# Down products of a feed-forward accumulated in shared PSUM banks, two token tiles at a time

## The chip, the cores and the metric

One Trainium2 chip, one core of it. The metric is the device time of one execution in microseconds (us), as the median of several runs. In rows and text PE is the matrix engine, DVE the vector engine, ACT the scalar engine, POOL GpSimd, and SP the queue that issues the transfers. PSUM is the memory that PE writes its sums to, in banks of 512 fp32 columns; SBUF is the working memory.

## The reference

The program is a two-layer network over 512 tokens of 1024 features and 256 context tokens. Each layer has a feed-forward, a mixer and a second feed-forward. The part that the change touches is the feed-forward:

```python
def swiglu(h, wg, wu, wd):
    return (jax.nn.silu(h @ wg) * (h @ wu)) @ wd

def sublayer_in(h, m, i):
    return h * (1.0 + m[..., i, 1, :]) + m[..., i, 0, :]

def residual(h, sub, m, i, g, b):
    return layer_norm(DEEPNORM_ALPHA * h + (1.0 + m[..., i, 2, :]) * sub, g, b)
...
        x_new = residual(x, 0.5 * swiglu(sublayer_in(x, m_l, 0), ffn_w_gate[l, 0], ffn_w_up[l, 0], ffn_w_down[l, 0]),
                         m_l, 0, norm_g[l, 0], norm_b[l, 0])
```

wg and wu are [1024, 2816], wd is [2816, 1024]; all of it is fp32.

## The kernel before

Tokens lie in tiles of 128: six tiles (four of the tokens, two of the context) in the first three feed-forwards, four in the last one, which drops the context. The 2816 inner features are worked in 11 *pairs* of 128 columns, and the pairs in five *groups* (GROUPS, L355): four groups of two pairs and a last one of three. For each pair, `gate_up` (L476) computes gate and up products, then the activations; after the last pair of a group, `down_blocks` (L705) multiplies the activations of its two pairs by the down weights and adds the result to `acc`, an fp32 accumulator [128, 1024] for each token tile in SBUF. The last group goes through `down_last` (L768), which the change leaves alone.

Every fp32 operand is held as two fp16 pieces, and a product is three matmuls (PASSES, L33). Weights are split by `split_weight` (L319): one ACT instruction for the first piece, one DVE instruction for the second. Activations are split the same way in `put_act` (L429; L445 on ACT, L446 on DVE).

Gate, up and down products use Winograd's form of Strassen's scheme. For the down products, the activations are cut in blocks (half of the tokens, column tile) and the weights in blocks (column tile, half of the 1024 output features). Sums of blocks are made on POOL beforehand (L391 to L394 for the down weights, L414 to L417 for gate and up weights, L437 to L440 for the activations). Seven block products, numbered 1 to 7, then give the four blocks of the result. With u2 = P1 + P6, u3 = u2 + P7 and u4 = u2 + P5, these are c11 = P1 + P2, c12 = u4 + P3, c21 = u3 - P4 and c22 = u3 + P5. A *tile step* covers a token tile of the first half and its partner in the second half, so a six-tile sublayer has three tile steps in a group and a four-tile one two.

In a tile step each product is six matmuls of 512 columns (two pairs, three passes) into a bank `pd` (L715) of the pool "sm", which has two banks. P1 is copied to SBUF by ACT (`D1`, L737). The sums u2, u3 and u4 are DVE additions of a bank to an SBUF buffer (`D`, L726). In the first group `put` writes each accumulator quarter once by DVE (L731). In the other groups it adds the bank by DVE (L733) and then the SBUF part by POOL (L734).

PSUM has three pools of two buffers each: "sm" (one bank each; down products, the conditioning matmuls of `ada_vec` at L162, and small things), "pf" (one bank each; gate and up products 4, 6 and 7, tiles `m`) and "big" (two banks each; gate and up products 1, 2, 3 and 5, tiles `x1` and `x2`).

Weight blocks go through a ring of 16 + 5 buffers, seven for each load of one pair's gate, up or down weights, three loads ahead (`prepare`, L803). A buffer is filled again once PE has read its block for the last time.

The order of instructions on each engine is not the source order. A scheduler lays the instructions out by readiness, subject to which buffers are free; each engine then runs its own row of instructions in that order. So a matmul whose bank is free can be laid ahead of one whose operands are still to come.

Of the kernel before, what the change touches and what calls it, by code (L numbers as in the profile page):

```python
# [15 lines left out]
P = 128  # L16
D = 1024
# [26 lines left out]
def kernel(  # L44
# [19 lines left out]
    def sm(shape, name):  # L64
        return ps.tile(shape, F32, tag="sm", name=name, bufs=2)
# [4 lines left out]
    class Tags:  # L70
        """Allocators of one phase: a rotating set of buffers for each kind of use."""
# [36 lines left out]
    def condition(alloc):  # L108
        """Loads the vectors that the whole network needs as columns, and takes them to columns."""
# [39 lines left out]
        # ALPHA times the gains and biases of the norms, as rows in DRAM  # L149
# [5 lines left out]
    def ada_vec(l, v, alloc):  # L155
        """One conditioning vector of both streams."""
# [42 lines left out]
    def affine_cols(l, i, prev):  # L199
        """Columns (scale, bias) that take the normalised rows to SA * (input of sublayer (l, i))."""  # L200
# [11 lines left out]
    def to_pieces(dst, src32):  # L212
        """src32 [P, KC, P] fp32 -> dst [P, 2, KC, P] fp16 pieces."""
# [3 lines left out]
    def turn(yh, t, cols, nm, alloc):  # L217
        """Rows of tile t -> transposed fp32 input of a sublayer, in two halves of its features."""
# [22 lines left out]
    class Stream:  # L241
        """The residual stream between sublayers: ALPHA times its rows in DRAM (the first one's without ALPHA), and
        the sublayer's transposed input where that is wanted again."""
# [6 lines left out]
    class Norm:  # L250
        """The normalisation that ends sublayer (l, i), and what follows from it, tile by tile in two stages."""
# [13 lines left out]
        def one(self, t, rt):  # L265
            """rt: the residual sum of tile t."""
# [45 lines left out]
    def block(shape, nm, dt=F16):  # L312
        """Room for the fp16 pieces of 512 weight columns (in several row tiles) or so."""
# [9 lines left out]
    class Pieces:  # L323
        """Pieces of a weight block, two row tiles in each buffer."""
# [7 lines left out]
    def load_raw(src, a, b, nm):  # L332
        """src may be a list of blocks that lie side by side."""
# [16 lines left out]
    # Gate and up products go by Winograd's form of Strassen's 2 x 2 x 2 scheme: with W^T in blocks A11, A12, A21, A22  # L350
    # (column tile, half of the features) and the input in B11, B12, B21, B22 (half of the features, half of the
    # tokens), seven block products of fp16 pieces give the four blocks of W^T u.
    # The down products of all but the last group of pairs go the same way: activations in blocks (half of the tokens,
    # column tile), weights in blocks (column tile, half of the output features).
    GROUPS = [[0, 1], [2, 3], [4, 5], [6, 7], [8, 9, 10]]  # L355

    def ffn(l, i, uT, stream, ntiles, nxt, last, todo):
# [5 lines left out]
        with tc.tile_pool(name=f"ffn{l}{i}", bufs=1) as fp:  # L363
# [8 lines left out]
            def ring(shape, nm):  # L372
                """A block of pieces from the two sets of buffers in turn, in proportion to their numbers."""
# [8 lines left out]
            def prep_down(pr_):  # L382
# [6 lines left out]
                else:  # L389
# [4 lines left out]
                    G.tensor_tensor(out=t4, in0=t2, in1=b21, op=ALU.subtract)  # L394
# [34 lines left out]
            def put_act(pr_, sg, spare):  # L429
                """Pieces of the activations sg of a pair, in blocks as its down products want them."""  # L430
# [17 lines left out]
            # differences of the input's blocks, as pieces  # L448
            tt = {}

            def differences(b11, b12, b21, b22, k, cols, shape, nm):
                """Blocks k, columns cols of the differences, from the fp32 input."""
# [23 lines left out]
            def gate_up(pr_):  # L476
# [5 lines left out]
                for q, dst in enumerate((sg, up)):  # L482
# [22 lines left out]
                    # the first pair leaves time for the differences, the last one starts with the first tokens  # L505
# [1168 lines left out]
```

## Time and profile before

| | us |
|---|---|
| median of 3 runs | 3025.64 |
| lowest and highest run | 3025.62, 3031.76 |
| span of the profiled execution, first to last instruction | 3023.2 |
| PE busy (all matmuls) | 2666.6 |
| DVE busy | 2538.8 |
| POOL busy | 1544.6 |
| ACT busy | 1224.7 |

The profile comes from one execution, and the profiled execution's own time is known as its span alone; the median of the runs lies 2.4 us above it. A row of the groups reads: line, engine, operation, output <- inputs, shapes, count, then busy time in us and mean ns of one, then the idle time of that engine just before them and what ended it. A row of the timeline gives start, length, engine, line and tile, with the idle time before it in brackets. Tile names carry no buffer numbers. In the span the first feed-forward runs until about 620 us, the second from 1095 to 1620, the third from 1690 to 2150 and the last from 2560 to the end; the mixers lie between.

### The profile page before, as it was taken

The numbers are of one execution on the slowest core, as the hardware profiler recorded it, in microseconds if no ns is written. First come the engines' busy times: TensorE is split into PE (matmuls) and PEld (weight loads), VectorE is DVE, ScalarE is ACT, GpSimd is POOL, SyncE is SP. The second block draws the span as 40 slices with busy tenths as digits, with TensorE's granted clock in tenths as the row PEclk, the third lists the DMA queues.
The fourth block names the chain that finished last, engine by engine and source line by source line (L and its number), as shares of the span: only waits on it lengthen the run. The fifth ranks groups of instructions, "written<-read, shape, count | busy, mean of one in ns | idle before, by whom it ended". The sixth has DMA issues, their size and how long they took to land. (4 is left out here: it accounts for less than half of the span.)

```text
span 3023.2 us, 45096 instructions
## 1 busy us (share of the span) xinstructions
PE 2666.6 (88%) x17087; PEld 1615.5 (53%) x17087; DVE 2538.8 (84%) x3677; ACT 1224.7 (41%) x2602; POOL 1544.6 (51%) x1296
## 2 busy tenths in 40 slices
PE   6799999989899979999999889888999998777778
PEld 4444444557677834444444444444556677555455
DVE  4988888886867788898789988898887777899998
ACT  3443343434447343343233443343335374444332
POOL 1646557132525464566725646567232444656672
PEclk9899999999999999999999999999999999899999
DMA  7253354333233253453372322122333342322222
GB/s 230 70 176 124 112 189 147 104 116 92 72 96 99 100 180 117 134 195 120 111 244 104 133 70 68 45 84 94 105 113 112 91 112 92 133 83 84 70 79 89
DMA packets 221519, 346.97 MB, mean 115 GB/s; under 512 B 16136, under 2 KB 162294, under 8 KB 221302
## 3 DMA queue, kind: packets, MB, share of 16 engines
q1 hardware_dynamic: 221302, 344.09, 35.3%
q8 instruction: 134, 2.20, 0.3%
q14 instruction: 83, 0.68, 0.1%
HBM read 303.52 MB, written 25.31 MB: 109 GB/s over the span
## 5 line engine op out<-in xcount | busy, mean ns | idle before, releaser
L494 PEld LDWEIGHTS <-pcgu 128*128 128x128 f16 x5088 | 500.4, 100 | 440.4 <-issue 181.2
L494 PE MATMUL m<-T,pcgu 128*128 128x384 f16 (+1 forms) x2400 | 410.7, 318 | 43.5 <-DVE U L499 31.1
L719 PE MATMUL pd<-pcd,act 128*128 128x512 f16 x1452 | 367.0, 392 | 76.9 <-DVE act L446 23.1
L719 PEld LDWEIGHTS <-act 128*128 128x128 f16 x1848 | 183.3, 100 | 343.2 <-issue 112.1
L494 PE MATMUL x<-uT,pcgu 128*128 128x384 f16 (+1 forms) x1512 | 254.8, 318 | 39.3 <-DVE sg L499 16.7
L321 DVE SCALAR_TENSOR_TENSOR pcgu<-rawgu,pcgu 128x512 f16<-128x512 f32 x208 | 237.6, 1156 | 16.6 <-ACT pcgu L320 16.4
L734 POOL TENSOR_TENSOR acc<-acc,D 128x512 f32<-128x512 f32 x132 | 188.9, 1443 | 71.0 <-DVE acc L733 70.6
L494 PEld LDWEIGHTS <-pegu 128*128 128x128 f16 x1632 | 160.4, 100 | 118.2 <-issue 36.0
L417 POOL TENSOR_TENSOR S4gu<-rawgu,S2gu 128x512 f32<-128x512 f32 x80 | 113.4, 1417 | 181.5 <-DVE pcgu L321 178.3
L414 POOL TENSOR_TENSOR S1gu<-rawgu 128x512 f32<-128x512 f32 x80 | 115.9, 1449 | 109.0 <-DMA rawgu<-in_ffn_w_gate_dram 55.5
L415 POOL TENSOR_TENSOR S2gu<-S1gu,rawgu 128x512 f32<-128x512 f32 x80 | 119.8, 1497 | 89.2 <-DVE pcgu L321 72.8
L416 POOL TENSOR_TENSOR S3gu<-rawgu 128x512 f32<-128x512 f32 x80 | 123.2, 1540 | 77.9 <-DVE pegu L321 54.5
L320 ACT ACTIVATE pcgu<-rawgu 128x512 f16<-128x512 f32 x208 | 125.6, 623 | 65.3 <-PE m L494 18.6
L942 PEld LDWEIGHTS <-uT 128*128 128x128 f16 x1344 | 133.7, 100 | 32.8 <-issue 12.6
L781 PE MATMUL pd<-pcd,act 128*128 128x512 f16 x594 | 144.7, 379 | 4.2 <-DVE dt L787 3.8
L94 POOL TENSOR_SCALAR rs<-mv 128x1 f32<-128x1 f32 x32 | 16.3, 508 | 240.5 <-DVE mv L273 240.5
L228 ACT ACTIVATE u<-pt,abc 128x128 f32<-128x128 f32 x224 | 81.5, 467 | 141.3 <-PE pt L225 95.5
L321 DVE SCALAR_TENSOR_TENSOR pcd<-rawd,pcd 128x512 f16<-128x512 f32 x132 | 135.4, 1039 | 0.8 <-ACT pcd L320 0.5
L446 DVE TENSOR_TENSOR act<-sg,act 128x384 f16<-128x384 f32 (+1 forms) x141 | 131.4, 963 | 2.2 <-ACT act L445 2.2
L781 PEld LDWEIGHTS <-act 128*128 128x128 f16 x792 | 77.4, 98 | 99.4 <-issue 12.6
L494 PE MATMUL x<-T,pcgu 128*128 128x384 f16 (+1 forms) x672 | 119.6, 320 | 11.8 <-DVE sg L499 6.5
L726 DVE TENSOR_TENSOR D<-D,pd 128x512 f32<-128x512 f32 x132 | 89.9, 681 | 46.6 <-PE pd L719 45.1
(375 smaller groups left out, 6403.5 us busy)
## 6 DMA issues: line engine op xcount, KB each, us to landing
adaw<-in_ada_w_dram SPq DMA_DIRECT2D x128, 512.0 KB
rawd<-in_ffn_w_down_dram SPq DMA_DIRECT2D x44, 1024.0 KB
rawgu<-in_ffn_w_gate_dram SPq DMA_DIRECT2D x43, 1024.0 KB
rawgu<-in_ffn_w_up_dram SPq DMA_DIRECT2D x43, 1024.0 KB
row<-yh SPq DMA_DIRECT2D x56, 256.0 KB
rawwo<-in_w_out_dram SPq DMA_DIRECT2D x8, 1024.0 KB
inp<-u SPq DMA_DIRECT2D x16, 512.0 KB
u<-inp SPq DMA_DIRECT2D x16, 512.0 KB
```

Source lines behind the costliest of these rows:

```text
L320: A.activation(pc[:, 0], src, AF.Copy, scale=SW)
L321: V.scalar_tensor_tensor(out=pc[:, 1], in0=src, scalar=SW, in1=pc[:, 0], op0=ALU.mult, op1=ALU.subtract)
L414: G.tensor_tensor(out=s1, in0=a21, in1=a22, op=ALU.add)
L415: G.tensor_tensor(out=s2, in0=s1, in1=a11, op=ALU.subtract)
L416: G.tensor_tensor(out=s3, in0=a11, in1=a21, op=ALU.subtract)
L417: G.tensor_tensor(out=s4, in0=a12, in1=s2, op=ALU.subtract)
L446: V.tensor_tensor(out=pc[:, 1], in0=src, in1=pc[:, 0], op=ALU.subtract)
L494: PE.matmul(pp, lhsT=blocks[m][:, a, k, :], rhs=rhs, start=(n == 0), stop=(n == 11))
L719: PE.matmul(pd, lhsT=acts[q][m][:, a, ts], rhs=wd[q][m][:, b], start=(n == 0), stop=(n == len(prs) * 3 - 1))
L734: G.tensor_tensor(out=c_, in0=c_, in1=part, op=ALU.add)
L781: PE.matmul(pd, lhsT=acts[q][2 * cc + hf][:, a, o:o + P], rhs=wd[q][2 * cc + h][:, b], start=(n == 0), stop=(n == len(prs) * 6 - 1))
L942: PE.matmul(pp, lhsT=uT[:, a, k, t * P:(t + 1) * P], rhs=pc.at(b, k, 0, n_), start=(n == 0), stop=(n == KC * 3 - 1))
```

## The change

A tile step now uses one bank `dc` ("chain", from the pool "pf") and one buffer of two banks `ds` ("side", from the pool "big"). Product 1 starts the chain bank, and products 6, 7 and 4 accumulate on top of it in PSUM, so that it holds P1, then u2, u3 and finally the last state in turn. Product 2 has the first side bank to itself; product 5 starts the second one, and product 3 accumulates on it. Each state is added by one DVE instruction to the accumulator quarter that needs it. That makes seven additions from PSUM into `acc`, and no addition by POOL. In the first group the first state that reaches a quarter is copied by ACT instead. The fourth sum of weight blocks changes sign, so that P4 can be accumulated.

Before a product can accumulate on a bank, the state in it must have been read. So tile steps run two at a time, product by product in turn, in the order 1, 2, 6, 5, 7, 3, 4. An odd third tile step runs by itself, in the order 1, 2, 5, 6, 3, 7, 4. "sm" is left to the conditioning matmuls. The diff also blanks comments, which is not shown.

```diff
@@ prep_down
-                    G.tensor_tensor(out=t4, in0=t2, in1=b21, op=ALU.subtract)
+                    G.tensor_tensor(out=t4, in0=b21, in1=t2, op=ALU.subtract)
@@ down_blocks
-                for t in range(ht):
+                reads = {1: ("c11",), 2: ("c11",), 6: ("c12",), 5: ("c22",), 7: ("c22",), 3: ("c12",), 4: ("c21",)}
+
+                def tile_products(t):
                     ts = slice(t * P, (t + 1) * P)
-                    def product(m):
-                        pd = sm([P, 512], f"pd{nm}{m}")
+                    chain = pf([P, 512], f"dc{nm}")
+                    side = big([P, 2, 512], f"ds{nm}")
+                    written = set() if gi == 0 else set(c)
+
+                    def step(m):
+                        pd = {2: side[:, 0, :], 5: side[:, 1, :], 3: side[:, 1, :]}.get(m, chain)
                         n = 0
                         for q in prs:
                             for a, b in PASSES:
                                 PE.matmul(pd, lhsT=acts[q][m][:, a, ts], rhs=wd[q][m][:, b],
-                                          start=(n == 0), stop=(n == len(prs) * 3 - 1))
+                                          start=(n == 0 and m in (1, 2, 5)), stop=(n == len(prs) * 3 - 1),
+                                          skip_group_check=m != 2)
                                 n += 1
-                        return pd
-                    def put(c_, part, m, op=ALU.add):
-                        if gi == 0:
-                            V.tensor_tensor(out=c_, in0=part, in1=m, op=op)
-                        else:
-                            V.tensor_tensor(out=c_, in0=c_, in1=m, op=op)
-                            G.tensor_tensor(out=c_, in0=c_, in1=part, op=ALU.add)
-                    m1 = ft("pt", [P, 512], f"D1{nm}")
-                    A.copy(m1, product(1))
-                    put(c11, m1, product(2))
-                    u2 = add(m1, product(6), 2)
-                    u3 = add(u2, product(7), 3)
-                    m5 = product(5)
-                    u4 = add(u2, m5, 4)
-                    put(c22, u3, m5)
-                    put(c12, u4, product(3))
-                    put(c21, u3, product(4), ALU.subtract)
+                        for key in reads[m]:
+                            if key in written:
+                                V.tensor_tensor(out=c[key], in0=c[key], in1=pd, op=ALU.add)
+                            else:
+                                A.copy(c[key], pd)
+                                written.add(key)
+
+                for t0 in range(0, ht, 2):
+                    steps_ = [tile_products(t) for t in range(t0, min(t0 + 2, ht))]
+                    for m in (1, 2, 6, 5, 7, 3, 4) if len(steps_) == 2 else (1, 2, 5, 6, 3, 7, 4):
+                        for step in steps_:
+                            step(m)
```

The scheduler moves a good deal with it. First PE's row in the third feed-forward, third group (pairs 4 and 5), around the hand-over from the gate and up products to the down stage. The name x210_51 is a bank of sublayer (1, 0), pair 5, up products; x110_60, m610_60, m710_60 and x210_60 belong to the next pair, 6; pd10_201 is group 2 (counted from 0), tile step 0, product 1; pcd10_5_1 and act10_5_1 are pair 5's weights and activations of product 1. Weight loads and further matmuls of the same kind are left out. Before:

```order
L494 MATMUL x210_51_18654<-uT02_15850,pegu10_513_18454 128x384
...
L494 MATMUL x110_60_19049<-uT02_15850,pcgu10_601_18767 128x384
...
L494 MATMUL m610_60_19077<-T210_16406,pcgu10_606_18773 128x384
...
L494 MATMUL m710_60_19092<-T310_16407,pcgu10_607_18776 128x384
...
L494 MATMUL x210_60_19107<-T110_16405,pcgu10_605_18779 128x384
...
L719 MATMUL pd10_201_18789<-pcd10_5_1_18736,act10_5_1_18705 128x512
...
L719 MATMUL pd10_202_18797<-pcd10_5_2_18739,act10_5_2_18708 128x512
...
L719 MATMUL pd10_206_18806<-pcd10_4_6_18479,act10_4_6_18420 128x512
```

And now, where dc10_20 and dc10_21 are the chain banks of tile steps 0 and 1, and ds10_20 and ds10_21 their side banks:

```order
L494 MATMUL x210_51_18270<-uT02_15538,pegu10_513_18070 128x384
...
L726 MATMUL dc10_21_18406<-pcd10_4_1_18086,act10_4_1_18024 128x512
...
L726 MATMUL ds10_21_18407<-pcd10_4_2_18089,act10_4_2_18027 128x512
...
L726 MATMUL dc10_20_18404<-pcd10_5_1_18352,act10_5_1_18321 128x512
...
L726 MATMUL dc10_21_18406<-pcd10_5_1_18352,act10_5_1_18321 128x512
...
L726 MATMUL ds10_20_18405<-pcd10_5_2_18355,act10_5_2_18324 128x512
...
L726 MATMUL dc10_20_18404<-pcd10_4_6_18095,act10_4_6_18036 128x512
...
L494 MATMUL x110_60_18623<-uT02_15538,pcgu10_601_18383 128x384
```

The next pair's gate products, which stood ahead of the first down product that needs pair 5's activations, now begin only when the two paired tile steps are nearly through; the third tile step lies among them. In their old place stand the products of pair 4 into four banks.

Then POOL's row in the last feed-forward, second group (tiles acc12_0 to acc12_3; S4gu12_41 is a sum of weight blocks for pair 4's up products, S1gu12_50 and the like for pair 5's gate products). Before:

```order
L417 TENSOR_TENSOR S4gu12_41_26952<-rawgu12_41_26947,S2gu12_41_26950 128x512
L734 TENSOR_TENSOR acc12_0_25738<-acc12_0_25738,D112_10_26817 128x512
L414 TENSOR_TENSOR S1gu12_50_26980<-rawgu12_50_26978 128x512
L734 TENSOR_TENSOR acc12_2_25740<-acc12_2_25740,D312_10_26851 128x512
L734 TENSOR_TENSOR acc12_0_25738<-acc12_0_25738,D412_10_26860 128x512
L734 TENSOR_TENSOR acc12_2_25740<-acc12_2_25740,D312_10_26851 128x512
L415 TENSOR_TENSOR S2gu12_50_26981<-S1gu12_50_26980,rawgu12_50_26978 128x512
```

And now:

```order
L417 TENSOR_TENSOR S4gu12_41_26436<-rawgu12_41_26431,S2gu12_41_26434 128x512
L414 TENSOR_TENSOR S1gu12_50_26464<-rawgu12_50_26462 128x512
L415 TENSOR_TENSOR S2gu12_50_26465<-S1gu12_50_26464,rawgu12_50_26462 128x512
L416 TENSOR_TENSOR S3gu12_50_26466<-rawgu12_50_26462 128x512
L417 TENSOR_TENSOR S4gu12_50_26467<-rawgu12_50_26462,S2gu12_50_26465 128x512
```

The additions into acc are gone from the row, and the sums for the next weights follow each other.

More of the change, by code (lines that the diff above doesn't have):

```diff
@@ L707, in down_blocks @@
                 ht = ntiles // 2
-                for t in range(ht):
+                reads = {1: ("c11",), 2: ("c11",), 6: ("c12",), 5: ("c22",), 7: ("c22",), 3: ("c12",), 4: ("c21",)}
+                def tile_products(t):
                     ts = slice(t * P, (t + 1) * P)
                     nm = f"{l}{i}_{gi}{t}"
-                    c11, c12, c21, c22 = (acc[t + r * ht][:, h * 512:(h + 1) * 512]
-                                          for r in range(2) for h in range(2))
-                    def product(m):
-                        pd = sm([P, 512], f"pd{nm}{m}")
+                    c = {f"c{r + 1}{h + 1}": acc[t + r * ht][:, h * 512:(h + 1) * 512]
+                         for r in range(2) for h in range(2)}
+                    chain = pf([P, 512], f"dc{nm}")
[3 more added lines that the diff above has]
+                        pd = {2: side[:, 0, :], 5: side[:, 1, :], 3: side[:, 1, :]}.get(m, chain)
                         n = 0
@@ L719, in product @@
                                 PE.matmul(pd, lhsT=acts[q][m][:, a, ts], rhs=wd[q][m][:, b],
-                                          start=(n == 0), stop=(n == len(prs) * 3 - 1))
+                                          start=(n == 0 and m in (1, 2, 5)), stop=(n == len(prs) * 3 - 1),
+                                          skip_group_check=m != 2)
                                 n += 1
-                        return pd
-                    def add(x_, y_, nm_):
-                        r_ = ft("pt", [P, 512], f"D{nm_}{nm}")
-                        V.tensor_tensor(out=r_, in0=x_, in1=y_, op=ALU.add)
-                        return r_
-                    def put(c_, part, m, op=ALU.add):
-                        if gi == 0:
-                            V.tensor_tensor(out=c_, in0=part, in1=m, op=op)
-                        else:
-                            V.tensor_tensor(out=c_, in0=c_, in1=m, op=op)
-                            G.tensor_tensor(out=c_, in0=c_, in1=part, op=ALU.add)
-                    m1 = ft("pt", [P, 512], f"D1{nm}")
-                    A.copy(m1, product(1))
-                    put(c11, m1, product(2))
-                    u2 = add(m1, product(6), 2)
-                    u3 = add(u2, product(7), 3)
-                    m5 = product(5)
-                    u4 = add(u2, m5, 4)
-                    put(c22, u3, m5)
-                    put(c12, u4, product(3))
-                    put(c21, u3, product(4), ALU.subtract)
+                        for key in reads[m]:
[4 more added lines that the diff above has]
+                                written.add(key)
+                    return step
+                for t0 in range(0, ht, 2):
[3 more added lines that the diff above has]
+                            step(m)
             def gate_rows_of(h):
```

## The prediction

> **What bounds the kernel now.** I read the page first, then stages, then the down products' groups and their waits, last one hand-over in the timeline. The page's first part:
>
> ```profile
> PE 2666.6 (88%) x17087; PEld 1615.5 (53%) x17087; DVE 2538.8 (84%) x3677; ACT 1224.7 (41%) x2602; POOL 1544.6 (51%) x1296
> ```
>
> PE and DVE lie close together and POOL is half idle. That is an average over mixers and feed-forwards, so next busy time by stage (length, then PE, PEld, DVE, ACT, POOL, granted clock, DMA). The first row is one period of the third feed-forward (six token tiles): two pairs of gate and up products and one down stage. The others are the first three periods of the last feed-forward (four tiles).
>
> ```profile
> 1922.00:2018.00 96.00, 85.70 (x450) 44.81 (x449) 86.73 (x107) 35.99 (x65) 60.69 (x43) 0.95 0.21 66
> 2653.00:2736.00 83.00, 63.95 (x427) 42.81 (x426) 78.14 (x106) 33.86 (x66) 46.19 (x34) 0.93 0.25 76
> 2736.00:2819.60 83.60, 63.30 (x422) 42.82 (x422) 77.87 (x104) 33.47 (x66) 55.34 (x40) 0.93 0.24 76
> 2819.60:2902.50 82.90, 63.23 (x419) 42.83 (x418) 77.50 (x102) 33.70 (x66) 56.70 (x41) 0.91 0.24 77
> ```
>
> In the six-tile period PE (85.7 of 96) and DVE (86.7) are equally full: each waits for the other in turn. In the last feed-forward DVE alone is the limit (78 of 83, PE 64). The down products' groups:
>
> ```profile
> L719 PE MATMUL pd<-pcd,act 128*128 128x512 f16 x1452 | 367.0, 392 | 76.9 <-DVE act L446 23.1 <-DVE acc L733 21.0 <-ACT D L737 14.8
> L734 POOL TENSOR_TENSOR acc<-acc,D 128x512 f32<-128x512 f32 x132 | 188.9, 1443 | 71.0 <-DVE acc L733 70.6 <-ACT act L445 0.2
> L726 DVE TENSOR_TENSOR D<-D,pd 128x512 f32<-128x512 f32 x132 | 89.9, 681 | 46.6 <-PE pd L719 45.1
> L733 DVE TENSOR_TENSOR acc<-acc,pd 128x512 f32<-128x512 f32 x132 | 89.7, 680 | 36.8 <-PE pd L719 36.6
> L731 DVE TENSOR_TENSOR acc<-D,pd 128x512 f32<-128x512 f32 x44 | 29.9, 680 | 11.9 <-PE pd L719 11.9
> L737 ACT COPY D<-pd 128x512 f32<-128x512 f32 x44 | 25.6, 582 | 132.1 <-PE pd L719 132.0
> ```
>
> There are 44 tile steps: three six-tile sublayers with 3 steps in each of four groups, and the last with 2. DVE stood 45.1 + 36.6 + 11.9 = 93.6 us waiting for a down product. The other direction, PE waiting for a `pd` bank to be read, is a row of the view of that tile (us, times), under "who waited for it":
>
> ```profile
>   PE pd L719: 54.9, 67
> ```
>
> **The change part by part.** Gains are negative.
>
> *POOL's adds.* The 132 adds of L734 (188.9 us of POOL) go. The last feed-forward prices them: its first period (83.0) has almost none, since the first group writes acc with L731, and the two after it have eight each; they take 83.6 and 82.9. POOL falls by 9 to 10.5 us there, the period by at most 0.6. On the chain that ended last they do show:
>
> ```profile
> 2833.86 3.37 POOL acc L734 x2
> ```
>
> At 3.4 us in each of the 12 groups that have them (three in each sublayer), 41 us would be the most. I take the period rows, which hold everything: 0.5 x 12 = **-6**, range -41 to 0.
>
> *DVE's reads.* In groups 2 to 4 a tile step had seven DVE instructions (three L726, four L733) and has seven adds into acc now, each again with one PSUM and one SBUF input of 512: nothing at 0.68. In the first group the first write of each of a step's four quarters becomes an ACT copy: 11 steps x 4 x 0.680 = 29.9 us of DVE go. ACT pays nothing in sum: its 44 copies of L737 go, 44 come. Half of it lies where DVE sets the pace: **-15**, range -30 to +15, the loss because those copies now stand behind ACT's weight splits, and L737 has already held PE for 14.8 us.
>
> *Bank waits.* A `pd` bank came round after one product between; a chain or side bank now comes round after three products of the pair, its own tile's and the other's. The 54.9 us can go. Where PE and DVE are equally full a PE wait counts half: **-27**, range -55 to 0. The odd third tile has as little as one product between, but its steps lie between gate products.
>
> *What leaves the hand-over.* The down stage now takes its banks from the two pools that gate and up products use. Here PE, in the third feed-forward, between the last product of a pair (x<-uT,pegu, 1925.41) and the down products that need that pair's activations:
>
> ```profile
> 1923.30 1.14 PE L494 MATMUL m<-T,pcgu 128*128 128x384 f16 x6
> 1924.28 1.30 PE L494 MATMUL x<-uT,pcgu 128*128 128x384 f16 x7
> 1925.41 2.11 PE L494 MATMUL x<-uT,pegu 128*128 128x384 f16 x12
> 1927.36 0.98 PE L494 MATMUL x<-uT,pcgu 128*128 128x384 f16 x5
> 1928.18 3.09 PE L494 MATMUL m<-T,pcgu 128*128 128x384 f16 x18
> 1931.10 1.79 PE L494 MATMUL x<-T,pcgu 128*128 128x384 f16 x10
> ...
> 1936.79 1.24 PE L719 MATMUL pd<-pcd,act 128*128 128x512 f16 x5 [2.28 <-ACT D L737]
> ...
> 1940.33 1.44 PE L719 MATMUL pd<-pcd,act 128*128 128x512 f16 x3 [1.52 <-DVE acc L733]
> 1941.56 2.94 PE L719 MATMUL pd<-ped,act 128*128 128x512 f16 x6
> ```
>
> Apart from the 12 of the old pair, these gate matmuls belong to the next pair, 48 of them with two stragglers not shown; 12 take 1.95 us (1925.41 to 1927.36), so 48 take 7.8 us. By the order of the changed program none of them stands there any more. Meanwhile the activations come late and one by one from DVE:
>
> ```profile
> 1931.04 4.16 DVE L446 TENSOR_TENSOR act<-sg,act 128x384 f16<-128x384 f32 x3
> 1940.80 1.61 DVE L446 TENSOR_TENSOR act<-up,act 128x384 f16<-128x384 f32 x1
> ```
>
> So PE would stand from 1927.4 to about 1932.4, where the first activation is ready. Three things give time back. The 13 next-pair matmuls ahead of the old pair's last product (rows 1923.30 and 1924.28, 2.1 us) no longer hold it and its activations up. The part that needs only the group's first pair is four products of three matmuls instead of two (six more; at 1.24 us for five with their tail, about 1.3). And each activation that arrives feeds two tiles, so the spell up to 1942.4 is fuller. 7.8 - 2.1 - 1.3 leaves 4.4, the pairing takes an estimated half: about 2 us a group, 24 in the 12 six-tile groups, half on the path: **+12**. In the last feed-forward DVE sets the pace: nothing. From below 0; from above all 7.8 in 12 groups, +94.
>
> A standstill has a second price. After 2.98 us without work the same 24 matmuls took 5.74 us, after 1.01 us 4.17:
>
> ```profile
> 1893.69 5.74 PE L494 MATMUL x<-uT,pcgu 128*128 128x384 f16 x24 [2.98 <-DVE up L499]
> 1910.41 4.17 PE L494 MATMUL x<-uT,pcgu 128*128 128x384 f16 x24 [1.01 <-DVE sg L499]
> ```
>
> That is 1.6 us for each such standstill, 19 us for 12 groups; the hand-over of before pays it too (six matmuls in 2.94 at 1941.56), so half: **+10**, range 0 to +19. [...]
>
> *Weight blocks and conditioning.* In the four-tile sublayer a product's weights are free once both tiles have had it, one product later, where before the second tile had them only after the whole first; DVE idles 5 us a period there, and I take 1.5 in each of four: **-6**, range -20 to 0. The conditioning vectors (L162) no longer share their PSUM pool with down products and move ahead in PE's order, some into the start, where PE is mostly idle:
>
> ```profile
> 60.00:80.00 20.00, 7.61 (x23) 3.67 (x24) 20.00 (x30) 11.00 (x23) 12.83 (x11) 0.60 0.01 1
> ```
>
> I take **-5**, range -15 to +5, the loss because their loads stand earlier in SP's queue, between the weight loads. The flipped sign of the fourth weight sum costs nothing: the same POOL subtraction.
>
> Sum: -6 - 15 - 27 + 12 + 10 - 6 - 5 = -37. DVE's and PE's savings partly buy the same time in the six-tile sublayers, so I take -35. The profiled span is 3023.2 us, and the median of the runs, 3025.64, lies 2.4 above: 3023.2 - 35 + 2.4 = 2990.6, say 2990.
>
> **The rivals.**
>
> *Slower: the hand-over.* PE sets the pace in the six-tile sublayers, and the uncovered spell counts in full: 7 us in 12 groups and the slow clock, 84 + 19 = 103, against 27 + 15 + 6 + 6 + 5 = 59. Net +44, and +20 if the pairing gives back 2 us a group: 3045 to 3070, say 3055. It decides once a group loses more than 59 / 12, about 5 us, clock included. For: PE is 89% busy there, and the spell is certain from the order. Against: DVE is 90% busy, and PE loses time to it in gate products (2.98 at 1893.69) that a later PE wouldn't lose. Chance 0.20.
>
> *No change.* DVE's queue is the limit, its work in groups 2 to 4 is the same, and what it saves in the first group reappears as waits for PE: 3020 to 3031. For: the three periods of the last feed-forward agree within 0.7 whether POOL adds or not. Chance 0.12.
>
> *Much faster: alternation was the cost.* PE's 54.9 us go in full, and a third of DVE's 93.6 (31) with the first group's 15: -100 with no loss at the hand-over, 2925 to 2960. Against: the same hand-over. Chance 0.12.
>
> *Faster by all of POOL.* Some DVE instructions are slowed by POOL: two neighbours, same operation and shape,
>
> ```profile
> 1929.03 0.68 DVE L321 SCALAR_TENSOR_TENSOR pegu<-S4gu,pegu 128x512 f16<-128x512 f32 x1
> 1929.63 1.48 DVE L321 SCALAR_TENSOR_TENSOR pcgu<-rawgu,pcgu 128x512 f16<-128x512 f32 x1
> ```
>
> If excluding each other set the end of every period, all 188.9 us would come off: about 2837. [...] Chance 0.02.
>
> **How the numbers follow.** My forecast, 2965 to 3015, has 0.54. About 0.2% (6 us) is what this kernel's measurement can tell from no change. Faster: 0.54 + 0.12 + 0.02 = 0.68; same: 0.12, less the half of it that could fall just outside, plus the weak edge of the hand-over rival: 0.11; slower: 0.21. The range takes most of the alternation case (from 2945) and the hand-over rival's lower half (to 3045); left out are about 0.10 above and 0.07 below.
>
> **What would show it.** The profile after should have no POOL adds into acc, 44 ACT copies into acc, PE's waits for a down bank under 20 us, and a PE idle of 3 to 6 us before the second half of each group's first product, released by L446. If the six-tile periods fall under 94 us and the last sublayer's first period falls most, the steps hold. I am wrong if that idle with its slow matmuls exceeds 5 us in most groups, if PE stands behind ACT's copies in the first groups, or if PE's waits move into the next pair's products, whose banks the down stage holds.

## The result and the profile after

The changed kernel takes 2955.52 us (median of 4 runs, 2952.61 to 2960.7), the kernel before 3027.14 in the same session. The ratio is 0.9769, 95% interval 0.9754 to 0.9784. In microseconds of a 3026 us run that is -70, with an interval of -74 to -65. The forecast, -35, had the direction and half of the size.

First the engines, from the page after:

```profile
span 2950.8 us, 45010 instructions
PE 2655.0 (90%) x17087; PEld 1623.2 (55%) x17087; DVE 2444.3 (83%) x3633; ACT 1227.8 (42%) x2602; POOL 1343.7 (46%) x1164
```

The span fell by 72.4 us, DVE's busy time by 94.5, POOL's by 200.9. DVE has 44 instructions fewer, the first writes that ACT now makes, which is 29.9 us; the other 65 us are instructions that became shorter. Summed over all its forms, the weight split L321 took 991 us in the trace before and 942 now.

The stages after, in the columns of the table before: a six-tile period, then the first three periods of the last feed-forward.

```profile
1894.80:1989.90 95.10, 86.27 (x463) 45.63 (x462) 82.44 (x110) 35.62 (x64) 44.30 (x33) 0.96 0.21 67
2605.00:2678.60 73.60, 61.23 (x421) 42.41 (x420) 69.19 (x96) 35.93 (x72) 42.87 (x34) 0.93 0.29 93
2678.60:2751.80 73.20, 61.64 (x422) 42.49 (x420) 71.30 (x102) 32.34 (x64) 41.52 (x33) 0.93 0.26 87
2751.80:2825.40 73.60, 60.94 (x419) 42.60 (x420) 71.91 (x104) 32.72 (x64) 42.12 (x34) 0.93 0.27 87
```

The four-tile periods lost nearly 10 us each: DVE's busy time went from about 78 to about 71, and its idle time from 5 or 6 us to 2 or 4. The six-tile period shown lost 0.9. In the down products' groups,

```profile
L732 DVE TENSOR_TENSOR acc<-acc,dc 128x512 f32<-128x512 f32 x143 | 95.1, 680 | 40.5 <-PE dc L726 40.5
L732 DVE TENSOR_TENSOR acc<-acc,ds 128x512 f32<-128x512 f32 x121 | 81.1, 679 | 46.1 <-PE ds L726 45.8
```

DVE now stands 40.5 + 45.8 = 86.3 us for a down product (93.6 before). The other way round, under "who waited for it", of the tile `dc` first and of `ds` second:

```profile
  PE dc L726: 19.7, 10
  DVE acc L732: 40.5, 55
...
  PE ds L726: 4.9, 4
```

PE's waits for a bank fell from 54.9 to 24.6 us. The hand-over in the third feed-forward, in PE's timeline:

```profile
1887.16 2.11 PE L494 MATMUL x<-uT,pegu 128*128 128x384 f16 x12
1889.11 0.81 PE L726 MATMUL dc<-pcd,act 128*128 128x512 f16 x3
1890.26 0.81 PE L726 MATMUL ds<-pcd,act 128*128 128x512 f16 x3 [0.34 <-DVE up L499]
1891.80 1.04 PE L726 MATMUL dc<-pcd,act 128*128 128x512 f16 x4 [0.73 <-ACT act L445]
...
1894.40 0.60 PE L726 MATMUL ds<-pcd,act 128*128 128x512 f16 x2 [0.27 <-DVE act L446]
1897.80 2.72 PE L726 MATMUL dc<-pcd,act 128*128 128x512 f16 x6 [2.79 <-DVE acc L732]
```

Without the next pair's matmuls to cover it, PE idles 0.34 + 0.73 + 0.27 + 2.79 = 4.1 us here. Before, with them, it idled 2.28 + 0.17 + 1.52 = 4.0 in the same place (the 0.17 in a row between those that the prediction shows). The uncovered spell isn't there: the paired steps fill it. The banks that the two stages now share cost little, too: the next pair's products wait 0.2 us for a chain bank and 1.5 for a side bank.

One balance is used for the stages. DVE is near its limit in every feed-forward (busy 86, 86, 90 and 92% of the stretches before), so I cut out four stretches: in the first three feed-forwards from the end of the first group's down products to the end of the last group's, in the last one from its first gate matmul to the same end. Their length is DVE's busy plus its idle time. The sum rows of the windows view (length, busy time of each engine, means), before:

```profile
sum 1777.30, PE 1573.95 PEld 861.67 DVE 1573.02 ACT 668.55 POOL 1009.44; mean PE 393.49 PEld 215.42 DVE 393.26 ACT 167.14 POOL 252.36
```

and after:

```profile
sum 1693.70, PE 1540.65 PEld 860.49 DVE 1491.20 ACT 652.75 POOL 818.83; mean PE 385.16 PEld 215.12 DVE 372.80 ACT 163.19 POOL 204.71
```

The stretches are 83.6 us shorter, and DVE is busy 81.8 us less; its idle time is 204.3 before and 202.5 after. But the two cuts don't hold the same work: by the counts of the same view DVE has 42 instructions fewer in them after the change (2114 and 2072), of which only 8 have left the program, the first writes of the last feed-forward; the others now lie outside the cuts. The whole program is free of this. There DVE is busy 94.5 us less and idle 22.1 us more (484.4 before, 506.5 after, the span less the busy time). The 29.9 us of writes that went to ACT bring no time by themselves (the third experiment below): idle time stands in their place. So some 65 of the 72 us are shorter DVE instructions, and the other 8 are idle time. The experiments show that this net hides more, since parts of it cancel.

### The profile page after: what moved, and what is told of

Same layout as the page of the kernel before. It is cut to its first block, busy times and chain, and to the rows that moved or that the text cites. A ratio compares the mean times of both kernels' runs of the same rounds, so it can differ in the third digit from the quotient of the medians.

```text
span 2950.8 us, 45010 instructions
## 1 busy us (share of the span) xinstructions
PE 2655.0 (90%) x17087; PEld 1623.2 (55%) x17087; DVE 2444.3 (83%) x3633; ACT 1227.8 (42%) x2602; POOL 1343.7 (46%) x1164
## 5 line engine op out<-in xcount | busy, mean ns | idle before, releaser
L726 PE MATMUL dc<-pcd,act 128*128 128x512 f16 x792 | 221.2, 401 | 35.9 <-DVE acc L732 19.5
L321 DVE SCALAR_TENSOR_TENSOR pcgu<-rawgu,pcgu 128x512 f16<-128x512 f32 x208 | 225.1, 1089 | 28.0 <-ACT pcgu L320 27.6
L726 PE MATMUL ds<-pcd,act 128*128 128x512 f16 x660 | 173.1, 385 | 14.2 <-DVE up L499 9.7
L779 PE MATMUL pd<-pcd,act 128*128 128x512 f16 x594 | 148.4, 381 | 3.5 <-DVE dt L785 3.5
L321 DVE SCALAR_TENSOR_TENSOR pcd<-rawd,pcd 128x512 f16<-128x512 f32 x132 | 135.2, 1033 | 6.2 <-ACT pcd L320 6.0
L446 DVE TENSOR_TENSOR act<-sg,act 128x384 f16<-128x384 f32 (+1 forms) x141 | 132.9, 982 | 5.4 <-ACT act L445 5.3
L732 DVE TENSOR_TENSOR acc<-acc,dc 128x512 f32<-128x512 f32 x143 | 95.1, 680 | 40.5 <-PE dc L726 40.5
L94 POOL TENSOR_SCALAR rs<-mv 128x1 f32<-128x1 f32 x32 | 15.2, 475 | 247.7 <-DVE mv L273 247.7
L732 DVE TENSOR_TENSOR acc<-acc,ds 128x512 f32<-128x512 f32 x121 | 81.1, 679 | 46.1 <-PE ds L726 45.8
```

The lines of the kernel that those rows point to most:

```text
L321: V.scalar_tensor_tensor(out=pc[:, 1], in0=src, scalar=SW, in1=pc[:, 0], op0=ALU.mult, op1=ALU.subtract)
L446: V.tensor_tensor(out=pc[:, 1], in0=src, in1=pc[:, 0], op=ALU.subtract)
L726: PE.matmul(pd, lhsT=acts[q][m][:, a, ts], rhs=wd[q][m][:, b], start=(n == 0 and m in (1, 2, 5)), stop=(n == len(prs) * 3 - 1), skip_group ...
L732: V.tensor_tensor(out=c[key], in0=c[key], in1=pd, op=ALU.add)
L779: PE.matmul(pd, lhsT=acts[q][2 * cc + hf][:, a, o:o + P], rhs=wd[q][2 * cc + h][:, b], start=(n == 0), stop=(n == len(prs) * 6 - 1))
```

## The experiments

Theory D: DVE's time made the gain, through POOL's adds, which stretch DVE's instructions, and through the first group's writes. Theory B: banks and order made it, through fewer waits between PE and DVE. In the tables below "us" is (ratio - 1) x 3026, each from its own comparison with the kernel before; an interval is about 4 or 5 us to either side, so a difference of two rows is good to some 6 or 7.

**POOL does as many sums as before.** The changed kernel, with a POOL sum for each that was removed, from acc into a buffer that nobody reads (in this run's trace nothing waits for these sums, tile Z):

```diff
+                            if gi > 0 and m in (2, 7, 3, 4):
+                                scr = ft("pt", [P, 512], f"Z{nm}{m}")
+                                G.tensor_tensor(out=scr, in0=c[key], in1=c[key], op=ALU.add)
```

> The changed kernel with 132 additions of the old size put back on POOL: four in each tile step of groups 2 to 4, each reading an accumulator quarter and writing a buffer that nobody uses. Theory D (DVE's time: what was gained is the time by which POOL's adds stretched DVE, and the first group's writes that left DVE): at least half of the 72 us come back, 2985 to 3005. Theory B (banks and order: the gain is fewer bank waits, earlier free weight blocks and conditioning matmuls that moved): under 15 us come back, 2955 to 2970. The prediction's own term for POOL was 6 us.

Measured: 2973.71 us, ratio 0.9831 (0.9814 to 0.9847): 18 us of the 70 go back, less than D and a little more than B expected. Its stretches, with as many DVE instructions in them as after the change:

```profile
sum 1710.40, PE 1532.64 PEld 855.31 DVE 1536.63 ACT 648.81 POOL 1006.35; mean PE 383.16 PEld 213.83 DVE 384.16 ACT 162.20 POOL 251.59
```

DVE is busy 45.4 us longer than after the change, but idle 173.8, which is 28.7 less. Its timeline beside POOL's sums (those run from 2785.61 to 2790.95 and from 2792.18 to 2795.07):

```profile
2785.46 0.67 DVE L732 TENSOR_TENSOR acc<-acc,dc 128x512 f32<-128x512 f32 x1
2786.06 1.14 DVE L321 SCALAR_TENSOR_TENSOR pcgu<-S2gu,pcgu 128x512 f16<-128x512 f32 x1
2787.12 1.52 DVE L321 SCALAR_TENSOR_TENSOR pegu<-rawgu,pegu 128x512 f16<-128x512 f32 x1
2788.57 0.67 DVE L732 TENSOR_TENSOR acc<-acc,ds 128x512 f32<-128x512 f32 x1
```

```profile
2785.61 5.38 POOL L738 TENSOR_TENSOR Z<-acc 128x512 f32<-128x512 f32 x4
2790.95 1.26 POOL L417 TENSOR_TENSOR S4gu<-rawgu,S2gu 128x512 f32<-128x512 f32 x1
2792.18 2.93 POOL L738 TENSOR_TENSOR Z<-acc 128x512 f32<-128x512 f32 x2
```

POOL's effect on DVE shows here. L732 (one input from PSUM, one from SBUF) stays at 0.67 beside POOL. L321, with both inputs from SBUF, takes 1.14 to 1.52. In the trace after the change L321's instructions of 512 columns take 0.68 us in the mean of the 509 with no POOL instruction beside them, and 1.34 in the mean of the 104 beside which POOL is busy throughout; L732 takes 0.68 in the mean of either kind (148 and 47).

**One tile step at a time.** The sums and accumulating banks of the change, but both tiles of banks of a step from "big", which has two buffers, so that only one step is under way. Every step then has the order of the odd third one, 1, 2, 5, 6, 3, 7, 4:

```diff
-                    chain = pf([P, 512], f"dc{nm}")
+                    two = big([P, 2, 512], f"dc{nm}")
+                    chain = two[:, 0, :]
...
-                for t0 in range(0, ht, 2):
-                    steps_ = [tile_products(t) for t in range(t0, min(t0 + 2, ht))]
+                for t0 in range(ht):
+                    steps_ = [tile_products(t) for t in range(t0, t0 + 1)]
```

> The changed kernel with both bank buffers of the pool big taken by one tile step (chain, product 2 and products 5 and 3 in three banks of it), so that only one tile step is under way at a time, in the order 1, 2, 5, 6, 3, 7, 4. Accumulation in PSUM and POOL's rest stay. Theory B: 20 to 50 us are lost, 2975 to 3005, most of it in the last feed-forward, where weight blocks come free later. Theory D: at most 10 us, 2955 to 2965.

Measured: 3009.19 us, ratio 0.9946 (0.9929 to 0.9963): 54 us of the 70 are gone, past B's estimate, against D. The tiles `dc` and `ds`, who waited for them:

```profile
  DVE acc L733: 61.9, 70
...
  PE dc L727: 38.6, 25
...
  DVE acc L733: 86.6, 64
...
  PE ds L727: 29.5, 35
```

PE waits 68.1 us for banks and DVE 148.5 for products: each stands while the other works. Its span is 3005.8 us, and its page begins:

```profile
PE 2670.2 (89%) x17087; PEld 1622.5 (54%) x17087; DVE 2446.3 (81%) x3633; ACT 1223.5 (41%) x2602; POOL 1366.9 (45%) x1164
```

DVE is busy only 2.0 us longer than after the change, while the span is 55.0 us longer: all of it is idle time. With accumulating banks for one step only, the change would be worth 16 us, not 70. B expected most of the loss in the last feed-forward, where weight blocks come free later; from its first gate matmul (2563.8) to the end, only 15.5 of the 55 us lie there.

**The first group's writes on DVE.** The 44 copies go back to DVE:

```diff
-                                A.copy(c[key], pd)
+                                V.tensor_copy(c[key], pd)
```

> The changed kernel with the first group's 44 first writes of an accumulator quarter on DVE instead of ACT, a copy of 512 each. Theory D: DVE has 44 more instructions, some 0.6 to 0.68 us each, 26 to 30 us, and 15 to 30 of them show: 2970 to 2985. Theory B: under 8 us, 2955 to 2963.

Measured: 2957.21 us, ratio 0.9777 (0.9761 to 0.9792), not to be told from the change. The 44 copies cost DVE 0.679 us each, 29.9 in all, and the time nothing that these runs can show.

**The old sums in the new banks.** The kernel before, with its POOL adds and its D sums, but the products' banks from the pools of the change:

```diff
-                        pd = sm([P, 512], f"pd{nm}{m}")
+                        if m in (1, 5):
+                            sides[0] = big([P, 2, 512], f"pd{nm}{m}")
+                        pd = sides[0][:, int(m in (2, 3)), :] if m in (1, 2, 5, 3) else pf([P, 512], f"pd{nm}{m}")
```

> The kernel before with its seven products, sums in SBUF and POOL adds unchanged, but its banks taken from the pools big (products 1, 2, 5, 3) and pf (6, 7, 4): six banks instead of two, and the conditioning matmuls have sm to themselves. Theory B: 25 to 50 us faster than before, 2975 to 3000. Theory D: within 10 us of before, 3015 to 3035; the loss of the next pair's products at the hand-over may cost up to 10 of it.

Measured: 3003.69 us, ratio 0.9927 (0.9912 to 0.9942): -22, with whatever it loses at the hand-over, which it shares with the change. PE's waits for a down bank fall from 54.9 to 19.4 us. That lies between the two ranges, just short of B's. The banks alone are worth about a third of the change.

**Banks that leave the hand-over free.** Two ways to put the next pair's matmuls back ahead of the down products:

```diff
-                    chain = pf([P, 512], f"dc{nm}")
+                    chain = sm([P, 512], f"dc{nm}")
```

> The changed kernel with one edit: the bank of products 1, 6, 7, 4 comes from the third pool of banks, sm, and the second pool, pf, stays free at the hand-over from the products to the down products, so that 24 matmuls of the next pair's products 6 and 7 stand ahead of the down products again; the conditioning matmuls then share sm with the down products. Theory H (the hand-over, where the changed kernel's PE idles about 4 us in each group, still costs several us a group, and matmuls of the next pair would fill it): with some 20 groups 10 to 25 us faster than the changed kernel, 2930 to 2946. Rival theory N (the hand-over costs nothing that can be won: what PE does there early it lacks later, since DVE sets the period): within 6 us of it, 2950 to 2962. If conditioning in sm gets in the way of the down products (the prediction's term of -5 for moving it), up to 10 slower, 2956 to 2966.

```diff
-                    side = big([P, 2, 512], f"ds{nm}")
+                    side = sm([P, 512], f"ds{nm}")
...
-                        pd = {2: side[:, 0, :], 5: side[:, 1, :], 3: side[:, 1, :]}.get(m, chain)
+                        pd = side if m in (2, 5, 3) else chain
```

> The changed kernel with one edit: products 2, 5 and 3 of a tile step go one after the other into one bank of sm instead of two banks of big, so that big stays free at the hand-over and 36 matmuls of the next pair's products 1 and 2 stand ahead of the down products. Theory H: the idle stretch at the hand-over goes from about 4 us to under 1.5 in each six-tile group, 10 to 25 us faster than the changed kernel, 2930 to 2946. Theory N: within 6 us, 2950 to 2962. The price that could hide a gain: product 5 has to wait until product 2's bank has been read, so PE's waits for ds banks would rise above the 4.9 us of the changed kernel by some 10.

Measured: 2951.17 us, ratio 0.975 (0.9736 to 0.9765), and 2950.82, ratio 0.9753 (0.9737 to 0.9768). Both are 5 or 6 us below the change, inside the doubt of the comparison: rival N. In the first, PE's waits for the two banks rise from 24.6 to 46.6 us, which may hide a gain. In the second they are 29.8 (5.6 of them for a side bank), so little hides there. Where the change idles 4.1 us at the hand-over, the second idles 2.1:

```profile
1893.74 0.33 PE L494 MATMUL x<-uT,pegu 128*128 128x384 f16 x1
1896.15 2.75 PE L726 MATMUL dc<-pcd,act 128*128 128x512 f16 x12 [2.08 <-DVE acc L732]
```

Filling half of the hand-over brings almost nothing with 21 buffers, so its loss looks small. It wasn't tried again with 20 buffers, as some steps below were. That the conditioning matmuls share "sm" with the down products again shows no cost either, but 5 us could hide in the doubt.

**Another number of weight blocks.** One buffer fewer (20), and in a second kernel one more (22) with a temporary less. FIT, the number of loads prepared ahead, is 3 in both, as in the change:

```diff
-NEXTRA = 5
+NEXTRA = 4
...
-FIT = (NBLOCK + NEXTRA) // 7
+FIT = 3
```

> The changed kernel with one buffer for conditioned weight blocks fewer, 20 instead of 21. Theory W (what the pairing gains is that weight blocks come free earlier, so the number of buffers is what the DVE's preparation of the next blocks waits for): 10 to 25 us slower, 2966 to 2981, with ACT's waits for L320's buffers (153.9 us put to PE and DVE after the change, estimate from its rows 34.2 and 134.1) up by 15 or more. Theory P (the pairing gains because DVE's reading of a bank lies beside the other tile's matmuls): at most 5 us slower, 2954 to 2961.

```diff
-NEXTRA = 5
+NEXTRA = 6
...
-            ft = Tags(fp, act=14, ada=2, pcd=NEXTRA, xa=NT, bc=4, T=4, pt=6, sg=4)
+            ft = Tags(fp, act=14, ada=2, pcd=NEXTRA, xa=NT, bc=4, T=4, pt=5, sg=4)
```

> The changed kernel with one buffer for conditioned weight blocks more, 22, and one temporary of the feed-forward's pt ring fewer, 5. Theory W: 4 to 15 us faster, 2941 to 2952. Theory P: within 4 us, 2952 to 2960, or up to 10 slower if the smaller ring of temporaries makes POOL's sums ahead of the products wait.

Measured: 2931.78 us with 20, ratio 0.9688 (0.9672 to 0.9704), and 2935.02 with 22, ratio 0.9696 (0.9681 to 0.971). Both are over 20 us faster than the change. Neither theory had that: fewer buffers are not slower, and one more gains no more than one fewer. ACT's waits for weight buffers that the down products hold, 34.2 + 134.1 = 168.3 us after the change (the 153.9 of the expectation is a slip), are 37.0 + 91.2 = 128.2 with 20. The number of buffers is no capacity that the gain lives on, but 21 is a bad number for the changed kernel. The stretches with 20:

```profile
sum 1674.50, PE 1526.21 PEld 856.57 DVE 1498.73 ACT 650.70 POOL 817.14; mean PE 381.55 PEld 214.14 DVE 374.68 ACT 162.68 POOL 204.28
```

DVE is busy 7.5 us longer than after the change, and idle 175.8 instead of 202.5 (over the whole program 20 longer, and 42 less idle). It is idle 180.2 with 22 and 173.8 with POOL's sums put back, so some 22 to 29 us of idle DVE belong to the changed kernel with 21 buffers. The one of DVE's waits that differs most is that for an up product, 35.0 us after the change:

```profile
DVE up L499 <- PE x L494: 35.0, 19, 4.1
```

and with 20 buffers 17.8, the longest 2.2 instead of 4.1:

```profile
DVE up L499 <- PE x L494: 17.8, 20, 2.2
```

This row alone doesn't make the difference: DVE's wait for a gate product (sg) rises from 2.7 to 15.2 us.

**The same steps with 20 buffers.** If an edit's price can be hidden by such an accident, the prices above need a second measurement. Three of the kernels ran again with 20 buffers, the kernel before among them.

> The kernel before with 20 buffers for conditioned weight blocks instead of 21, the same edit as in e7, as a control: how far does the size of this ring move a time by itself, whatever way the sums are made? Theory A (the ring of 20 simply suits the feed-forward better): about 21 us faster than before, 3000 to 3012, and the change is then worth about 72 us again in this ring. Rival theory R (what an edit gives depends on how it reshuffles the order, so that the ring's gain belongs to the changed kernel alone): within 8 us of before, 3018 to 3034, or slower, and the change is worth 85 to 100 in this ring.

Measured: 3033.91 us, ratio 1.0028 (1.0018 to 1.0038), 8 us slower than before: theory R. The smaller ring is no gain in itself; the change is worth some 103 us in it, a little more than R gave.

> The edit of e1 (POOL does as many sums as before, into a buffer that nobody reads) on top of the ring of 20 of e7. Theory A (the edits' prices add): 18 us slower than e7, 2944 to 2956. Theory R (a difference of under 20 us between two of these kernels can be the order's alone): between 10 faster and 10 slower than e7 or over 30 slower, so that e1's 18 is no price of POOL's sums.

Measured: 2986.31 us, ratio 0.987 (0.9856 to 0.9885), 55 us slower than the same kernel without POOL's sums. That is R's second case: 18 was no price of POOL's sums. Its stretches:

```profile
sum 1726.70, PE 1541.72 PEld 862.57 DVE 1552.22 ACT 650.70 POOL 996.55; mean PE 385.43 PEld 215.64 DVE 388.05 ACT 162.68 POOL 249.14
```

Beside the row with 20 buffers above, with equally many DVE instructions, the stretches are 52.2 us longer; DVE is busy 53.5 us longer and idle 1.3 less.

> The edit of e4 (the kernel before with its own sums, products 6, 7, 4 into banks of pf and 1, 2, 5, 3 into big) on top of the ring of 20. Theory A: 24 us faster than the kernel before with 20 buffers, about 2976 to 2988. Theory R: within 10 us of the kernel before with 20 buffers, or over 40 faster, so that e4's 24 is the order's as much as the banks'.

Measured: 3006.58 us, ratio 0.9937 (0.9922 to 0.9952), 27 or 28 us faster than the kernel before with 20 buffers. This step repeats, as theory A has it.

Each kernel differs from the next by one step, so the change can be cut up twice:

```
us beside the kernel before                21 buffers   20 buffers
kernel before                                   0           +8
old sums, new banks                           -22          -19
accumulating, two steps, POOL's sums kept     -51          -39
the change                                    -70          -94

step                                       21 buffers   20 buffers
other banks                                   -22          -28
accumulating, two steps at a time             -29          -20
POOL's sums gone                              -19          -55
all                                           -70         -103
```

In DVE's balance over the whole program (busy time from the first line of each page, idle time as the span less it) the steps are not alike:

```
DVE busy + idle, us          21 buffers        20 buffers
kernel before             2538.8 + 484.4    2549.0 + 481.2
old sums, new banks       2539.3 + 459.6    2564.9 + 442.6
POOL's sums kept          2487.6 + 484.8    2517.1 + 470.1
the change                2444.3 + 506.5    2464.4 + 464.8
```

The first step takes idle time, 25 and 39 us, and no busy time (with 20 buffers it adds 16): that is the alternation of PE and DVE, theory B. The second takes 52 and 48 us of busy time, but 29.9 of them are the writes that went to ACT, and the idle time rises by 25 and 28 for them. What is left, 22 and 18 us of shorter instructions, is most of this step. L321 becomes 32 us shorter in it (1008 to 976 us, 21 buffers), and the time that it overlaps with POOL's instructions falls by as much, from 578 to 545. The third takes 43 and 53 us of busy time; its idle time rises by 22 with 21 buffers and falls by 5 with 20. So the second and third step are in the main DVE's time, theory D, though by the run with one step at a time the second can't be had without banks for two steps.

By place, from the traces: up to the first gate matmul of the last feed-forward the third step is -13.9 us with 21 buffers and -47.8 with 20; in the last feed-forward it is -7.7 and -10.2. So some 34 us of it stay away with 21 buffers ahead of the last feed-forward; that this is the idle DVE time above is likely, not shown.

> The edit of e2 (the changed kernel's sums and banks, one tile step at a time) on top of the ring of 20 of e7. Theory A: 54 us slower than e7, 2975 to 2997. Theory R: anything from 30 to 80 slower, 2962 to 3012; under 15 slower would say that the pairing's gain was an accident of the ring of 21.

The kernel that ran here had only half of the edit that this text names: the loop takes one tile step at a time, but the chain bank stays in "pf", so that the banks still allow two. Measured: 2937.94 us, ratio 0.9709 (0.9695 to 0.9724), 6 us slower than with the paired loop, within the doubt. So it tells nothing of theories A and R. It says that the loop's order is not what counts: with banks for two steps, PE's waits for a bank are 28.9 us, and 28.2 with the paired loop. What a single step's banks cost with 20 buffers wasn't measured.

## Why the prediction was half right

*POOL's adds.* This is the step that failed. The term was -6, within a range to -41; taking POOL's sums away is worth 19 us with 21 buffers and 55 with 20, and 45 to 54 of DVE's busy time in the stretches. The working took three periods of one run, of which the first has almost no adds, and found them equal. But these periods differ in more than the adds. The right comparison is the same periods with and without. The three between the ends of the down products in the last feed-forward add up after the change to

```profile
sum 224.80, PE 186.79 PEld 129.27 DVE 216.80 ACT 98.58 POOL 133.02; mean PE 62.26 PEld 43.09 DVE 72.27 ACT 32.86 POOL 44.34
```

and with POOL's sums put back to

```profile
sum 234.00, PE 182.38 PEld 124.74 DVE 228.23 ACT 98.19 POOL 160.00; mean PE 60.79 PEld 41.58 DVE 76.08 ACT 32.73 POOL 53.33
```

They are 9.2 us longer (0.6, 4.0 and 4.6), and DVE is busy 11.4 us longer. They hold 21 of the sums, 0.44 us for each. As an estimate all 132 would cost 58 us by that; the whole last feed-forward, 7.7 us for 24 sums, would make it 42. With 20 buffers the three periods are 8.7 us longer. The other end that the text kept, 3.4 us in each of 12 groups and 41 in all, was the better one. The sums that I put back are not the old ones: they delay no accumulator write but the next one, and took 1.27 us each, 1.44 in the kernel before. That the second step also takes 32 us from L321 suggests that the old sums cost more than these; it wasn't tried alone. The chance of 0.02 for the case by POOL goes with that reading.

*DVE's reads.* In place of -15, 1.7 us was measured, within the doubt. The copies lie in the first groups, and 29.9 us of DVE's work there did not set the pace. The counter-cost, PE behind ACT's copies, didn't come either: PE waits 0.4 us for them.

*Bank waits and hand-over.* The first step measures -22 and -28, and it holds the bank waits (-27) with the hand-over (+12), the slow clock (+10) and the conditioning (-5), -10 in sum. So the bank waits were right or too small, and most of the +22 did not come. "None of them stands there any more" was right of the order, but the spell of 4.4 us was not: PE idles 4.1 us at the hand-over shown, 4.0 before, and putting matmuls back there brought 5 or 6 us in all. The slow clock shows at the place (six matmuls in 2.72 us after, 2.94 before, the granted clock 0.50 in both), but it cost as much before: the granted clock in the four stretches is 0.99, 0.99, 0.97 and 0.92 before and 1.00, 0.98, 0.98 and 0.92 after. The reading of the odd third tile step was wrong: in its order 7 and 4 follow each other in the chain bank with no product between, not one. What the working did not see is the condition: the same sums with banks for one step only take 54 us more, in the one measurement of it.

*The two small terms of order.* Conditioning matmuls back in "sm" show no cost, so no run shows the -5, which is too small for these comparisons. The vectors had "sm" not quite to themselves either, since `down_last` still takes its banks there. The earlier weight blocks weren't tried alone; their sign that "the last sublayer's first period falls most" did not show: the periods fall by 9.4, 10.4 and 9.3.

*The rivals.* The hand-over case fell with its spell. "No change" rested on the same three periods as the -6. The result lies inside the alternation case, 2925 to 2960, but for another reason: alternation is worth 22 to 28 us, and PE's waits fell by 30, not by 54.9. It lies outside the forecast's own 2965 to 3015, and inside the wider range only because that was stretched to 2945 for this rival: that is luck. The case "faster by all of POOL" named what carries most, DVE instructions slowed beside POOL (L321 0.68 us without POOL, 1.34 with POOL busy throughout), and a price several times too large: 19 or 55 us against 188.9. What counts is how far POOL's time stretches DVE, not POOL's time itself; that the two exclude each other was not shown.

*The signs named.* No POOL adds and 44 ACT copies: yes. PE's bank waits under 20 us: 24.6. Six-tile periods under 94: mostly not; counted to the end of each down stage, those of groups 2 to 4 take 101 us in the mean of the second feed-forward and 94 in that of the third (102 and 97 before). An idle of 3 to 6 us released by L446 is not at the hand-over shown: the longest there is 2.79, released by L732. The four-tile sublayer gained more for each group: of the 72.4 us of span the last feed-forward gave 29.1 in its five groups, the rest of the program 43.3, with fifteen groups.

What stays open is why 21 buffers hold back the changed kernel alone. The extra waits are spread over several rows, the up products' the clearest, and 22 buffers are as good as 20; which block's reuse causes them wasn't tried. The version with 20 buffers, 2931.78 us, is the fastest of all that ran, and needs one buffer less than the change.

## What to carry to other kernels

A sum taken off a half-idle engine can be worth more than one taken off a busy one, if it slows the busy engine's instructions (here 19 or 55 us for 132 sums of POOL, and none that shows for 44 writes of DVE): price it by the same stage with and without it, not by two neighbouring stages. An accumulating PSUM bank that is read between its products wants banks for a second, independent sum beside it; here that was worth 54 us, and with the banks there the order of the loop made no difference to be told (6 us, within the doubt). A balance of busy and idle time needs cuts that hold the same instructions: count them. And before a price of some 20 us in 3000 is believed, measure the edit a second time in a kernel whose order has been shaken by something neutral, such as a ring's length.

## What the hardware showed unexpectedly

POOL's 132 sums cost DVE 45 to 54 us of busy time in the stretches. L321 alone took 34 us more with 21 buffers and 37 with 20, while L732 kept 0.68 us whether POOL worked or not.

After 2.79 us without work, six matmuls of 512 columns took 2.72 us at the third feed-forward's hand-over; with the side bank from "sm", twelve took 2.75 us after 2.08. But at the hand-over of the last feed-forward, where PE is less busy, ten took 4.00 us after 2.05, as PE's timeline after the change shows:

```profile
2681.53 4.00 PE L726 MATMUL dc<-pcd,act 128*128 128x512 f16 x10 [2.05 <-DVE acc L732]
```

The clock rows tell these apart. In the changed kernel's trace the granted clock changes only at the ends of steps of 3.41 us, and its changes go with how busy PE was in the whole step before. Length, then busy time of PE, PEld, DVE, ACT and POOL, then the clock, for the step with the last 2.05 us of standstill and the next one:

```profile
2678.56:2681.98 3.42, 1.37 (x7) 0.51 (x6) 3.42 (x5) 2.06 (x5) 1.35 (x2) 1.00 0.00 0
2681.98:2685.39 3.41, 3.41 (x10) 1.21 (x9) 3.41 (x6) 0.60 (x1) 2.01 (x2) 0.50 0.00 0
```

and with the side bank from "sm", for the step with the 2.08 us:

```profile
1894.30:1897.72 3.42, 1.57 (x8) 0.74 (x8) 3.42 (x7) 1.04 (x2) 0.18 (x1) 1.00 0.00 0
1897.72:1901.13 3.41, 3.41 (x18) 1.51 (x17) 3.41 (x7) 0.00 (x0) 0.00 (x0) 1.00 0.00 0
```

PE was busy 0.40 of the first step and the clock halved after it, when PE had already worked again for 0.45 us; it was busy 0.46 of the second and the clock stayed. Worked out from the clock and matmul records of the changed kernel's trace, from 100 us on: the 36 steps at full clock that the clock halved after had PE busy for at most 0.42, the 747 after which it stayed for at least 0.41; from half clock it came back after 35 steps of 0.77 or more and stayed at half after 15 of 0.765 or less. So in this trace it is PE's busy share of a whole step that goes with the change, not the last standstill's length.
